# A softmax mixture: the last four groups' stores in two queues, from a freed slot, with the last copy in two pieces

## The chip, the cores and the metric

The kernel runs on one core of a Trainium2 chip. The metric is device time in microseconds (us) of one execution. Three runs of the kernel before took 794.04, 794.33 and 794.41 us, a median of 794.33 us. The profile was taken of a further execution that took 794.6 us.

Five engines work beside each other, each through its own list of instructions in order: TensorE (PE, matrix products; PEld is its load of weights), VectorE (DVE), ScalarE (ACT), GpSimd (POOL) and SyncE (SP). SP does nothing here but issue transfers (DMAs); ACT can issue them too, between its own instructions. Transfers issued by SP show in the trace as queue q1, those issued by ACT as queue q10. "SPq" and "ACTq" are instructions of those two that issue or wait.

## The reference

For each of 32 x 128 = 4096 rows there are four heads of 4096 logits and four prior values. Each head goes through a softmax of its own, and the four are averaged with the softmax of the priors as weights:

```python
prior_probs = softmax(prior, axis=-1)                 # [32, 128, 4]
softmax_h   = softmax(logits, axis=-1)                # [32, 128, 4, 4096]
mixture     = (prior_probs[..., None] * softmax_h).sum(axis=2)   # [32, 128, 4096], float32
```

The logits are 268 MB and the output is 67 MB, all in float32.

## The kernel before

**Units and groups.** The 4096 rows are cut into 32 groups (g) of 128 rows, and each group into two units of 64 rows, so there are 64 units, n = 0 to 63. A unit's logits are one tile of 128 partitions by 2 x 4096 numbers, 4 MB: a row takes two partitions, and each partition holds two of the row's heads (i = 0 and 1).

**A unit's way through the engines.** `load(n)` (L62) brings the 4 MB into one of five slots, slot n % 5; only the last unit comes as two loads of 2 MB, one per i. `top(n, i)` (L72) lets DVE find the row maximum of 4096 numbers (L74) and ACT take the exponential in place and its sum (L77). `weigh(n, i)` (L81) lets DVE invert the sum, POOL build a 128 x 64 weight matrix (L84), and PE multiply it with the slot in eight products of 512 columns (L91). The two `weigh` of a unit add up in one PSUM accumulator, `accs[n % 2]`. Its 128 partitions are not 128 rows: partitions 0 to 63 hold columns 0 to 2047 of the 64 output rows (c = 0), and partitions 64 to 127 hold columns 2048 to 4095 of the same rows (c = 1). `evict(n)` (L105) is an ACT copy of 128 x 2048 from PSUM to the group's place in SBUF, and `store(g)` (L108) sends a group out as two DMAs of 1 MB, one for c = 0 and one for c = 1. So every store reads one half of the partitions.

**Order.** The scheduling is written out by hand. In the loop (L148) unit n's `top` calls come ahead of the rest of unit w = n - 1:

```python
top(n, 0);  weigh(w, 1);  load(w + 5)      # SP waits until PE has read the whole slot of unit w
top(n, 1);  weigh(n, 0);  evict(w)
store(w // 2)                              # if w is odd
```

**Where a group's output waits.** `home(g)` (L100) says where a group is copied to. Up to group 29 that is `obuf`, with a place for even and one for odd groups. Groups 30 and 31 go to slot 4, (N - 5) % 5, which no unit after 59 uses.

**Which queue.** Groups 0 to 27 are stored from ACT (L109, `HOLD` = 28), right after the copy of their second unit. The last four groups are stored from SP. Groups 28 and 29 are held back: their four stores stand on SP behind the last load (L159 to L163). Group 30's follow after unit 61's copy. Group 31 goes out in two parts, its first unit's rows after unit 62's copy (L166) and its second unit's after the last copy (L169), each as two DMAs of 512 KB. On SP the tail is therefore one line: load 62, load 63 in two halves, then 28 (c = 0, c = 1), 29, 30, 31 first unit, 31 second unit, always c = 0 ahead of c = 1.

Of the kernel before, what the change touches and what calls it, by code (L numbers as in the profile page):

```python
# [1 line left out]

# [4 lines left out]

FP32 = mybir.dt.float32
AF = mybir.ActivationFunctionType
ALU = mybir.AluOpType  # L10
AX = mybir.AxisListType

P = 128
M = 64
J = 2
Q = 2
BANK = 512
SLOTS = 5


@with_exitstack
def kernel(
    ctx: ExitStack,
    tc: tile.TileContext,
    logits: bass.AP,
    prior: bass.AP,
    out: bass.AP,
):
    nc = tc.nc
    B, S, H, V = logits.shape  # L30
    R = M * J
    G = B * S // R
    N = G * J
    W = V // 2
    assert G * R == B * S and G == 32 and H == 2 * Q and V == 8 * BANK


    lg = logits.rearrange("b s h v -> (b s) h v").rearrange(
        "(g m j) (q i) v -> g j m q (i v)", m=M, j=J, i=Q
    )  # L40
    ov = out.rearrange("b s v -> (b s) v").rearrange("(g m j) v -> g m j v", m=M, j=J)
    pv = prior.rearrange("b s h -> (b s) h").rearrange("(g r) h -> g r h", r=R)

    cpool = ctx.enter_context(tc.tile_pool(name="cpool", bufs=1))
    psum = ctx.enter_context(tc.tile_pool(name="psum", bufs=1, space=bass.MemoryType.PSUM))

    slots = [cpool.tile([P, Q, V], FP32, name=f"slot{i}") for i in range(SLOTS)]

    obuf = cpool.tile([P, 2, J, W], FP32, name="obuf")
    accs = [psum.tile([P, W], FP32, name=f"acc{i}") for i in range(2)]  # L50

    sel = cpool.tile([P, M], FP32, name="sel")
    wts = [[cpool.tile([P, M], FP32, name=f"wt{k}{i}") for i in range(Q)] for k in range(2)]
    pr = cpool.tile([G, R, H], FP32, name="pr")
    pn = cpool.tile([G, J, Q, M, Q], FP32, name="pn")
    pmax = cpool.tile([G, R], FP32, name="pmax")
    pp = cpool.tile([P, J, Q, G], FP32, name="pp")
    nmax = [cpool.tile([P, N], FP32, name=f"nmax{i}") for i in range(Q)]
    dsum = [cpool.tile([P, N], FP32, name=f"dsum{i}") for i in range(Q)]
    rden = [cpool.tile([P, N], FP32, name=f"rden{i}") for i in range(Q)]  # L60

    def load(n):  # L62
        src = lg[n // J, n % J]
        if n < N - 1:
            nc.sync.dma_start(out=slots[n % SLOTS], in_=src)  # L65
        else:
            for i in range(Q):
                nc.sync.dma_start(
                    out=slots[n % SLOTS][:, i], in_=src[:, :, i * V : (i + 1) * V]
                )  # L70

    def top(n, i):  # L72
        x = slots[n % SLOTS][:, i]
        nc.vector.tensor_reduce(  # L74
            out=nmax[i][:, n : n + 1], in_=x, axis=AX.X, op=ALU.max, negate=True
        )
        nc.scalar.activation(  # L77
            x, x, AF.Exp, bias=nmax[i][:, n : n + 1], accum_out=dsum[i][:, n : n + 1]
        )

    def weigh(n, i):  # L81
        nc.vector.reciprocal(rden[i][:, n : n + 1], dsum[i][:, n : n + 1])  # L82
        wt = wts[n % 2][i]
        nc.gpsimd.tensor_scalar(  # L84
            out=wt, in0=sel, scalar1=rden[i][:, n : n + 1],
            scalar2=pp[:, n % J, i, n // J : n // J + 1], op0=ALU.mult, op1=ALU.mult,
        )

        for b in range(W // BANK):
            for c in range(2):  # L90
                nc.tensor.matmul(  # L91
                    accs[n % 2][c * M : (c + 1) * M, b * BANK : (b + 1) * BANK],
                    lhsT=wt,
                    rhs=slots[n % SLOTS][:, i, c * W + b * BANK : c * W + (b + 1) * BANK],
                    start=i == 0, stop=i == Q - 1,
                )

    HOLD = G - 4

    def home(g):  # L100
        if g < G - 2:
            return obuf[:, g % 2]
        return slots[(N - 5) % SLOTS][:, g % 2].rearrange("p (j w) -> p j w", j=J)

    def evict(n):  # L105
        nc.scalar.copy(home(n // J)[:, n % J], accs[n % 2])  # L106

    def store(g, js=slice(0, J)):  # L108
        eng = nc.scalar if g < HOLD else nc.sync  # L109
        for c in range(2):  # L110
            eng.dma_start(
                out=ov[g, :, js, c * W : (c + 1) * W], in_=home(g)[c * M : (c + 1) * M, js]
            )

    with tc.manual_schedule():
        for n in range(SLOTS):
            load(n)
        nc.scalar.dma_start(out=pr, in_=pv)

        nc.gpsimd.memset(sel, 1.0)  # L120
        nc.gpsimd.affine_select(  # L121
            out=sel, in_=sel, compare_op=ALU.is_ge, fill=0.0, base=0,
            pattern=[[-Q, M]], channel_multiplier=1,
        )
        nc.gpsimd.affine_select(  # L125
            out=sel, in_=sel, compare_op=ALU.is_ge, fill=0.0, base=Q - 1,
            pattern=[[Q, M]], channel_multiplier=-1,
        )

        nc.vector.reduce_max(pmax, pr, axis=AX.X)  # L130
        nc.vector.tensor_sub(pr, pr, pmax.unsqueeze(2).to_broadcast([G, R, H]))  # L131
        nc.scalar.activation(pr, pr, AF.Exp)  # L132
        nc.vector.reduce_sum(pmax, pr, axis=AX.X)  # L133
        nc.vector.reciprocal(pmax, pmax)  # L134
        prv = pr.rearrange("g (m j) (q i) -> g j i m q", j=J, i=Q)
        pmv = pmax.rearrange("g (m j) -> g j m", j=J)
        for j in range(J):
            for i in range(Q):
                nc.vector.tensor_mul(  # L139
                    pn[:, j, i], prv[:, j, i], pmv[:, j].unsqueeze(2).to_broadcast([G, M, Q])  # L140
                )
        pq = pn.rearrange("g j i m q -> g j i (m q)")
        for t in range(P // 32):
            nc.vector.transpose(  # L144
                pp[32 * t : 32 * (t + 1)], pq[:, :, :, 32 * t : 32 * (t + 1)]
            )

        for n in range(N):  # L148
            w = n - 1
            top(n, 0)  # L150
            if w >= 0:
                weigh(w, 1)
                if w + SLOTS < N:
                    load(w + SLOTS)
            top(n, 1)
            weigh(n, 0)
            if w >= 0:
                evict(w)
                if w == N - SLOTS:  # L159
                    for g in range(HOLD, w // J):  # L160
                        store(g)
                if w % J == J - 1 and (w // J < HOLD or w >= N - SLOTS):
                    store(w // J)  # L163

        n = N - 1
        store(n // J, slice(0, 1))  # L166
        weigh(n, 1)
        evict(n)
        store(n // J, slice(1, 2))  # L169


# [1 line left out]
_INS = ['logits', 'prior']  # L173
_OUTS = [((32, 128, 4096), 'float32')]


# [23 lines left out]
```

## Time and profile before

| What | Value |
|---|---|
| median of three runs | 794.33 us |
| profiled execution, whole | 794.6 us |
| its span (first to last instruction) | 792.9 us |
| outside the span | 1.7 us |
| busiest engines, share of the span | ACT 76%, DVE 72%, PE 69% |
| bytes moved | 268.5 MB read, 67.1 MB written |
| landing of load 62, the last 4 MB load | 754.57 us |
| end of the last ACT copy | 782.79 us |

How to read it: times are microseconds from the start of the span. Where a row shows an instruction and "x4", four like it follow each other, and the duration is that from the first one's start to the last one's end. The "DMA share" of a stretch is the mean busy share of the core's 16 DMA engines in it; it comes out a little over 1.00 at times, because packets are counted where they start. "To landing" is the time from a DMA's issue until its completion is signalled. The trace also holds every DMA packet with its start, duration, size and queue; a load's packet is 32 KB (16 KB for the two half loads), a store's is 8 KB.

### The profile page before, as it was taken

What the parts mean: (1) busy time and instruction counts of PE and PEld (TensorE: products, weight loads), DVE (VectorE), ACT (ScalarE), POOL (GpSimd) and SP (SyncE); (2) the same over time, 40 slices, a digit from 0 to 9 for tenths busy, and PEclk for the clock granted to TensorE, in tenths of its full rate; (3) what the DMA queues carried; (4) which work ended last, traced back from release to release, by engine and by line L of the source; (5) the groups of instructions that cost most, each with busy time, mean ns of one, the idle gap of its engine ahead of it and who ended that gap; (6) DMA issues with size and microseconds to landing.
All of it is one profiled execution on the core that took longest, in us unless ns stands there. A gap on an engine that the chain in (4) does not pass through costs nothing.

```text
span 792.9 us, 5418 instructions
## 1 busy us (share of the span) xinstructions
PE 544.3 (69%) x2048; PEld 159.6 (20%) x2048; DVE 573.3 (72%) x268; ACT 600.1 (76%) x322; POOL 51.1 (6%) x135
## 2 busy tenths in 40 slices
PE   0766567687776687666866677768568687776773
PEld 0212112122221122121211221212112122222221
DVE  5986867767768668677687686776866867767890
ACT  1897777787787787777877778778778777787893
POOL 0000000000000000000000000000000000000000
PEclk9998998877898977999799899887998877998998
DMA  9999999999999999999999999999999999999997
GB/s 375 441 414 431 430 426 429 433 431 428 433 436 433 434 434 431 429 427 437 429 431 429 431 434 431 433 436 430 433 432 432 427 432 427 432 431 438 432 386 234
DMA packets 18681, 335.95 MB, mean 424 GB/s; under 512 B 2112, under 2 KB 2112, under 8 KB 2144
## 3 DMA queue, kind: packets, MB, share of 16 engines
q1 hardware_dynamic: 10544, 276.83, 81.9%
q10 hardware_dynamic: 8112, 58.79, 17.6%
q8 instruction: 16, 0.26, 0.1%
q14 instruction: 9, 0.07, 0.0%
HBM read 268.50 MB, written 67.11 MB: 423 GB/s over the span
## 4 chain that ended last, share of the span: by engine, by line
DMA 76%; PE 10%; DVE 10%; issue 1%; POOL 1%; ACT 1%; SPq 0%; POOLq 0%
DMA slot<-in_logits_dram 76%; PE acc L91 10%; DVE nmax L74 9%; POOL wt L84 1%; ACT slot L77 0%; ACT slot L106 0%; SPq L65 0%; DVE rden L82 0%; POOLq L84 0%
## 5 line engine op out<-in xcount | busy, mean ns | idle before, releaser
L91 PE MATMUL acc<-slot,wt 128*64 128x512 f32 x2048 | 544.3, 689 | 236.6 <-POOL wt L84 236.5
L74 DVE TENSOR_REDUCE nmax<-slot 128x1 f32<-128x4096 f32 x128 | 563.5, 4410 | 194.6 <-DMA slot<-in_logits_dram 194.6
L77 ACT ACTIVATE slot<-slot,nmax 128x4096 f32<-128x4096 f32 x128 | 474.6, 3708 | 177.1 <-DVE nmax L74 175.7
L91 PEld LDWEIGHTS acc<-slot,wt 128*64 128x64 f32 x2048 | 159.6, 157 | 620.4 <-POOL wt L84 315.4
L106 ACT COPY obuf<-acc 128x2048 f32<-128x2048 f32 x60 | 110.7, 1845 | 0.0
L84 POOL TENSOR_SCALAR wt<-sel,rden,pp 128x64 f32<-128x64 f32 x128 | 50.3, 393 | 725.3 <-DVE rden L82 725.3
L77 ACT ACTIVATION_READ_ACCUMULATOR slot<-slot,nmax 128x1 f32 x128 | 23.9, 187 | 0.0
L82 DVE RECIPROCAL rden<-dsum 128x1 f32<-128x1 f32 x128 | 19.6, 153 | 5.1 <-ACT slot L77 5.1
L106 ACT COPY slot<-acc 128x2048 f32<-128x2048 f32 x4 | 7.4, 1850 | 2.8 <-PE acc L91 2.8
L130 DVE TENSOR_REDUCE pmax<-pr 32x128 f32<-32x512 f32 x1 | 0.7, 673 | 2.7 <-DMA pr<-in_prior_dram 2.7
L132 ACT ACT_TABLE_LOAD x1 | 1.3, 1283 | 1.2 <-PEq L184 1.2
L132 ACT ACTIVATE pr<-pr 32x512 f32<-32x512 f32 x1 | 0.6, 629 | 1.6 <-DVE pr L131 1.6
L144 DVE STREAM_TRANSPOSE pp<-pn 32x128 f32<-32x128 f32 x4 | 1.2, 302 | 0.1
L133 DVE TENSOR_REDUCE pmax<-pr 32x128 f32<-32x512 f32 x1 | 0.7, 674 | 0.7 <-ACT pr L132 0.7
L134 DVE RECIPROCAL pmax<-pmax 32x128 f32<-32x128 f32 x1 | 0.9, 941 | 0.0
L139 DVE TENSOR_TENSOR pn<-pr,pmax 32x128 f32<-32x128 f32 x4 | 0.9, 274 | 0.0
L131 DVE TENSOR_TENSOR pr<-pr,pmax 32x512 f32<-32x512 f32 x1 | 0.7, 678 | 0.0
L121 POOL TENSOR_SCALAR_AFFINE_SELECT sel<-sel 128x64 f32<-128x64 f32 x1 | 0.2, 238 | 0.1
L125 POOL TENSOR_SCALAR_AFFINE_SELECT sel<-sel 128x64 f32<-128x64 f32 x1 | 0.2, 238 | 0.1
L120 POOL MEMSET sel<- 128x64 f32 x1 | 0.2, 151 | 0.3 <-POOLq L184 0.3
L184 POOL MEMSET const-float32-0.0<- 128x1 f32 x1 | 0.1, 98 | 0.3 <-issue 0.3
L184 POOL MEMSET const-bfloat16-1.0<- 128x1 bf16 x1 | 0.1, 101 | 0.0
(2 smaller groups left out, 0.2 us busy)
## 6 DMA issues: line engine op xcount, KB each, us to landing
slot<-in_logits_dram SPq DMA_DIRECT2D x63, 4096.0 KB, 38.0
out_dram<-obuf ACTq DMA_DIRECT2D x56, 1024.0 KB, 25.5
slot<-in_logits_dram SPq DMA_DIRECT2D x2, 2048.0 KB, 32.9
out_dram<-obuf SPq DMA_DIRECT2D x4, 1024.0 KB, 31.0
out_dram<-slot SPq DMA_DIRECT2D x2, 1024.0 KB, 15.5
out_dram<-slot SPq DMA_DIRECT2D x4, 512.0 KB, 9.2
pr<-in_prior_dram ACTq DMA_DIRECT2D x1, 64.0 KB, 1.8
```

The source lines that it names most:

```text
L74: nc.vector.tensor_reduce(out=nmax[i][:, n : n + 1], in_=x, axis=AX.X, op=ALU.max, negate=True)
L77: nc.scalar.activation(x, x, AF.Exp, bias=nmax[i][:, n : n + 1], accum_out=dsum[i][:, n : n + 1])
L82: nc.vector.reciprocal(rden[i][:, n : n + 1], dsum[i][:, n : n + 1])
L84: nc.gpsimd.tensor_scalar(out=wt, in0=sel, scalar1=rden[i][:, n : n + 1], scalar2=pp[:, n % J, i, n // J : n // J + 1], op0=ALU.mult, op1= ...
L91: nc.tensor.matmul(accs[n % 2][c * M : (c + 1) * M, b * BANK : (b + 1) * BANK], lhsT=wt, rhs=slots[n % SLOTS][:, i, c * W + b * BANK : c * ...
L106: nc.scalar.copy(home(n // J)[:, n % J], accs[n % 2])
L130: nc.vector.reduce_max(pmax, pr, axis=AX.X)
L131: nc.vector.tensor_sub(pr, pr, pmax.unsqueeze(2).to_broadcast([G, R, H]))
L132: nc.scalar.activation(pr, pr, AF.Exp)
L134: nc.vector.reciprocal(pmax, pmax)
L139: nc.vector.tensor_mul(pn[:, j, i], prv[:, j, i], pmv[:, j].unsqueeze(2).to_broadcast([G, M, Q]))
L144: nc.vector.transpose(pp[32 * t : 32 * (t + 1)], pq[:, :, :, 32 * t : 32 * (t + 1)])
```

## The change

It touches only the end of the kernel and the bookkeeping of slots.

1. **Four slots for the last six units.** Units 58 to 63 use the slots 4, 0, 1, 2, 4, 0. Before they used 3, 4, 0, 1, 2, 3. A load is issued once the unit that had its slot before is done (`prior_user`). Loads 58 to 63 thus wait for units 54 to 59, where they waited for 53 to 58.
2. **Homes.** Slot 3 is free after unit 53, and groups 28 and 29 are copied there. Groups 30 and 31 go to `obuf`. `obuf` has the same size as before under another shape.
3. **Two queues.** Each of the last stores' c = 0 halves goes out from SP and its c = 1 half from ACT. The c = 1 halves of groups 28 and 29 stand on ACT between `top(62, 0)` and `top(62, 1)`; their c = 0 halves stand on SP behind the last load. The halves of group 30 follow unit 61's copy, and those of group 31's first unit follow unit 62's copy. All of ACT's issues are in its own list: what stands behind them on ACT are the remaining exponentials and copies.
4. **The last copy in two pieces.** `evict(63)` is done as two ACT copies of 128 x 1024, and after each its columns are stored, 256 KB from SP and 256 KB from ACT.

In the built program ACT gains six DMA issues and one copy in its list, SP goes from ten DMAs behind the last load to six, all of them c = 0 halves, and PE, DVE and POOL keep their instructions and order. Each of the four final stores waits for one of the stores of groups 28 and 29 to complete, because it uses that store's completion semaphore again.

```diff
-    obuf = cpool.tile([P, 2, J, W], FP32, name="obuf")
+    obuf = cpool.tile([P, J, V], FP32, name="obuf")
...
+    def slot(n):
+        return slots[n % SLOTS if n < N - 6 else (4, 0, 1, 2)[(n - N + 6) % 4]]
...
+    def part(eng, g, c, js=slice(0, J), lo=0, hi=W):
+        eng.dma_start(
+            out=ov[g, :, js, c * W + lo : c * W + hi],
+            in_=home(g)[c * M : (c + 1) * M, js, lo:hi],
+        )
...
     def home(g):
-        if g < G - 2:
-            return obuf[:, g % 2]
-        return slots[(N - 5) % SLOTS][:, g % 2].rearrange("p (j w) -> p j w", j=J)
+        x = slots[3] if HOLD <= g < G - 2 else obuf
+        return x[:, g % 2].rearrange("p (j w) -> p j w", j=J)
-    def evict(n):
-        nc.scalar.copy(home(n // J)[:, n % J], accs[n % 2])
-    def store(g, js=slice(0, J)):
-        eng = nc.scalar if g < HOLD else nc.sync
+    def evict(n, lo=0, hi=W):
+        nc.scalar.copy(home(n // J)[:, n % J, lo:hi], accs[n % 2][:, lo:hi])
+    def store(g):
         for c in range(2):
-            eng.dma_start(
-                out=ov[g, :, js, c * W : (c + 1) * W], in_=home(g)[c * M : (c + 1) * M, js]
-            )
+            part(nc.scalar, g, c)
+    def prior_user(n):
+        return max(k for k in range(n) if slot(k) is slot(n))
...
             top(n, 0)
+            if n == N - 2:
+                for g in (HOLD, HOLD + 1):
+                    part(nc.scalar, g, 1)
             if w >= 0:
                 weigh(w, 1)
-                if w + SLOTS < N:
-                    load(w + SLOTS)
+                for k in range(SLOTS, N):
+                    if prior_user(k) == w:
+                        load(k)
+                if w == N - 3:
+                    for g in (HOLD, HOLD + 1):
+                        part(nc.sync, g, 0)
             top(n, 1)
             weigh(n, 0)
             if w >= 0:
                 evict(w)
-                if w == N - SLOTS:
-                    for g in range(HOLD, w // J):
-                        store(g)
-                if w % J == J - 1 and (w // J < HOLD or w >= N - SLOTS):
-                    store(w // J)
+                g = w // J
+                if w % J == J - 1 and g < HOLD:
+                    store(g)
+                elif w == N - 3 or w == N - 2:
+                    js = slice(0, J) if w == N - 3 else slice(0, 1)
+                    part(nc.sync, g, 0, js)
+                    part(nc.scalar, g, 1, js)
         n = N - 1
-        store(n // J, slice(0, 1))
         weigh(n, 1)
-        evict(n)
-        store(n // J, slice(1, 2))
+        for lo in (0, W // 2):
+            evict(n, lo, lo + W // 2)
+            part(nc.sync, n // J, 0, slice(1, 2), lo, lo + W // 2)
+            part(nc.scalar, n // J, 1, slice(1, 2), lo, lo + W // 2)
```

## The prediction, made before the changed kernel ran

> **What bounds the kernel now.** I read the page's 40 slices first, then its chain of the work that ended last.
>
> ```profile
> DMA  9999999999999999999999999999999999999997
> GB/s 375 441 414 431 430 426 429 433 431 428 433 436 433 434 434 431 429 427 437 429 431 429 431 434 431 433 436 430 433 432 432 427 432 427 432 431 438 432 386 234
> ...
> DMA 76%; PE 10%; DVE 10%; issue 1%; POOL 1%; ACT 1%; SPq 0%; POOLq 0%
> ```
>
> The DMA engines are busy throughout, at about 430 GB/s, and the chain is mostly loads. So the bytes set the time, and no change at the end can gain more than the end loses. It loses in the last two slices, 386 and 234 GB/s: with 19.8 us a slice, 19.8 x (1 - 386/432) + 19.8 x (1 - 234/432) = 2.1 + 9.1 = 11.2 us. The table of stretches shows how (the columns after ACT and POOL are PE clock, DMA share, GB/s).
>
> ```profile
> core 0: us, PE busy (x) PEld busy (x) DVE busy (x) ACT busy (x) POOL busy (x), PEclk, DMA share, GB/s
> 755.00:760.00 5.00, 3.33 (x18) 0.95 (x16) 5.00 (x3) 5.00 (x4) 0.39 (x1) 1.00 1.00 423
> ...
> 765.00:769.00 4.00, 3.27 (x18) 0.94 (x16) 4.00 (x3) 4.00 (x4) 0.39 (x1) 1.00 1.01 354
> 769.00:773.00 4.00, 3.15 (x16) 0.84 (x12) 3.33 (x2) 4.00 (x3) 0.00 (x0) 1.00 1.03 344
> 773.00:777.00 4.00, 3.47 (x16) 1.06 (x16) 0.17 (x1) 4.00 (x3) 0.62 (x2) 1.00 0.96 320
> 777.00:783.00 6.00, 3.84 (x18) 1.06 (x16) 0.00 (x0) 2.99 (x2) 0.17 (x1) 1.00 0.92 276
> 783.00:786.00 3.00, 0.00 (x0) 0.00 (x0) 0.00 (x0) 0.00 (x0) 0.00 (x0) 0.99 0.99 259
> 786.00:793.00 7.00, 0.00 (x0) 0.00 (x0) 0.00 (x0) 0.00 (x0) 0.00 (x0) 0.50 0.39 132
> ```
>
> From 765 us on the engines are as busy as before but move less: 354 falling to 259 GB/s. Only stores are left then. In the trace's packets the last load packet ends at 764.26 and the last store packet at 791.45. Of the 8.39 MB of the held groups 28 to 31, 0.66 MB has started by 764.26; the other 7.73 MB take 27.2 us, or **284 GB/s**. 27% of these 8 KB packets took over 500 ns, with a cluster near 630, twice the usual 309. Earlier, as store packets ran singly between load packets, 98% of 7168 took 312 ns or less. So packets get in each other's way when all engines read one half of the partitions at a time. The tail is bound by these stores: ACT is done at 782.79, and 8 us of stores follow.
>
> The compute path of the tail is ACT's list (start, duration, work, and in brackets the wait ahead of it):
>
> ```profile
> 759.18 3.71 ACT L77 ACTIVATE slot<-slot,nmax 128x4096 f32<-128x4096 f32 x1
> 762.79 0.19 ACT L77 ACTIVATION_READ_ACCUMULATOR slot<-slot,nmax 128x1 f32 x1
> 763.43 3.71 ACT L77 ACTIVATE slot<-slot,nmax 128x4096 f32<-128x4096 f32 x1 [0.45 <-DVE nmax L74]
> ...
> 767.14 1.84 ACT L106 COPY slot<-acc 128x2048 f32<-128x2048 f32 x1
> 768.89 3.71 ACT L77 ACTIVATE slot<-slot,nmax 128x4096 f32<-128x4096 f32 x1
> ...
> 776.28 1.84 ACT L106 COPY slot<-acc 128x2048 f32<-128x2048 f32 x1
> 780.92 1.87 ACT L106 COPY slot<-acc 128x2048 f32<-128x2048 f32 x1 [2.79 <-PE acc L91]
> ```
>
> These are units 62 and 63. From 763.43 to 776.28 ACT never waits, so whatever is put into its list there comes out at the end.
>
> **The change, part by part.**
>
> *Four slots: nothing.* Each load from 58 on is issued one unit later. In this trace load 62 is issued at 721.74, when unit 57 is done, and load 63's second half at 733.6, when unit 58 is. Afterwards load 62 goes at 733.6 and load 63's second half near 745. Loads land at 735.1, 744.9, 754.6 (units 60 to 62), so load 62's bytes start to flow at 744.9 and those of 63's second half near 759.9. The cover is 11 and 15 us of load already queued. If it were gone, each us short would cost a us. A gain is excluded, since no load goes earlier.
>
> *Homes: nothing.* Slot 3 is read last at 674.2 (unit 53), and its first copy comes after 711. `obuf`'s last ACT stores have landed by 733, its next copy comes at 757.
>
> *28 and 29 in two queues.* ACT issues two DMAs behind the exponential that ends at 762.98. Two such issues take 1.20 us in this kernel (the pair at 677.07). They end at 764.2 where the next exponential began at 763.43: **+0.8**. The trace shows no issue behind work it need not wait for. If ACT issues ahead, this is 0 and the stores may go as early as 749.5, when unit 59's copy ends; in four-to-one packet turns with the loads they would then hold up load 62 by some 1.1 us. Bounds 0 to +1.1. Issued at 763, they also share the engines with load 63's second half for its last 1.5 us; that half then lands near 766, and DVE reads it at 767.77, so this costs nothing.
>
> *30 on ACT.* The issue follows the copy that ends at 768.98 and pushes the last two exponentials: **+0.7** (0.60 and a hand-over). The spread of an issue is wide:
>
> ```profile
> L111 SPq DMA_DIRECT2D out_dram<-slot x6: 466/1231/2299, 769.0 to 783.3; - x6
> ```
>
> On SP in this very stretch three issues of the six, each the second of a pair, took 1.9 to 2.3 us. On ACT they would stand alone, so I take 0.6; the other end is 2.3, +1.7 more for group 30 and as much for the last copy's first piece. Group 31's first unit issues behind the copy that ends at 778.1, inside the 2.79 us wait: nothing, as long as it is shorter than that.
>
> *Copy in two pieces.* No half copy is in the trace. It costs between half of 1.87 and all of it; 4096 numbers take 3.71, 2048 take 1.85, so time goes by size and I take 1.0. PE's last product ends at 780.9 + 1.5 = 782.4. Piece one ends at 783.4, ACT's issue at 784.05, piece two at 785.05, against 782.79 before: **ACT ends 2.3 us later.**
>
> *The stores.* If two queues let packets of both halves alternate, they run at the 423 to 432 GB/s of the mixed stretches: 28 and 29 (4.19 MB) are through by 774.5, 30 (2.10 MB, ready at 770.4) by 779.5, 31's first unit (1.05 MB, issued at 779.7) by 784. The completions that the final stores wait for are those of 28 and 29: 774.5, or 779 at 284 GB/s, ahead of 783.4, so this wait, which on ACT has piece two behind it, costs nothing. Then nothing is in the way of the end: last issue 785.1; 1.45 us to its first packet (the kernel's first load: issue 0.80, packet 2.25); 0.52 MB in 1.2 us at 424 or 2.0 at 260, I take 1.7, and 0.3 for what piece one left: 788.5. From the last packet to the end of the span this trace has 792.9 - 791.45 = 1.45. **Span 789.95, or 2.95 us shorter.** The profiled execution becomes 794.6 - 2.95 = 791.65; the median stands 0.27 below it: **791.4 us.**
>
> [...] The trace's row is 284 GB/s for halves one behind the other. [...]
>
> **Rivals.**
>
> 1. *The queues gain little (same).* The stores still end last, at 270 to 300 GB/s, or ACT's issues take 2.3 us. At 300 the span is 764.3 + 25.8 + 1.45 = 791.5, at 270 it is 794.4, and with 3.4 us of slow issues on my forecast 793.3. With the 1.45 us between a span and the median (1.7 - 0.27) that is 792.9 to 795.8 us. For it: ACT's and SP's DMAs use the same 16 engines, and these are already at share 1.0. Against it: their packets are slow only when they meet.
> 2. *The halves meet in step (slower).* With strict turns, two engines that start on the same half stay on it together, packet after packet, where the single queue lets a fast engine run ahead to the other half. It decides below 284 GB/s (8192 bytes x 16 engines / 284 = a mean packet of 461 ns). At 250 GB/s the span is 764.3 + 30.9 + 1.45 = 796.6, so **798.1 us**; at 212, every packet at 618 ns, 803.6. For it: the rate sank toward 259 as the tail went on. Against it: in the steady part store packets took turns with load packets on all engines and hardly ever met.
> 3. *Loads run dry with four slots.* Against it are 11 us of cover; a gap of 3 us would end the gain at 794.4. Counted with the first.
>
> **How the numbers follow.** 0.2%, or 1.6 us, is about what a measurement of this kernel can tell from no change: 792.7 to 795.9. Forecast, 0.58: from 789.9 (pair hidden on ACT, 1.2 us transfer, nothing left of piece one) to 792.7. First rival, 0.17. Second, 0.25, from 795.9 to 803.6; I count some two fifths of it below 797. The range from 789.9 to 797 leaves out about 0.15 above and 0.03 below. The forecast's own range is 789.9 to 792.7.
>
> **What would show it.** Right: over 400 GB/s in the first 8 us after the last load packet, store packets at 309 ns, then gaps in the DMA share near 780; ACT's last piece ending near 785, and the last landing within 4 us of its issue. Slower rival: share near 1 to the end, packets of 500 to 630 ns on both queues. Wrong in the cheap parts: DVE waiting longer than 0.9 us for load 61 or 62, or an ACT gap over 1 us behind a DMA issue. The forecast is wrong if the last store packets wait behind others at 785.

## The result, and the profile after

Nine runs of the changed kernel took 790.95 to 793.28 us, a median of **792.9 us**; nine of the kernel before on the same chip had a median of 794.33. The ratio is **0.9974, 95% interval [0.9964, 0.9985]**: faster, by 1.4 us where 2.9 were forecast. The nine times fall in two groups, 790.95 to 792.08 (four runs) and 792.9 to 793.28 (five). The profiled execution took 793.28 us, so it is of the slower group; its span is 791.6 us, where 789.95 was forecast.

The page of the changed kernel, rates by slice (19.8 us each) and the chain of waits:

```profile
GB/s 376 442 416 431 431 428 430 432 431 427 434 432 435 429 432 436 430 433 431 434 429 433 431 431 429 428 435 431 429 431 432 431 432 433 433 430 436 429 416 229
...
DMA 73%; PE 12%; DVE 10%; ACT 2%; issue 1%; POOL 1%; ACTq 0%; SPq 0%; POOLq 0%
```

The slice before the last has risen from 386 to 416 GB/s, the last has stayed at 229 (234 before). In the chain DMA has lost 3% of the span and PE and ACT have gained it: the chain now leaves the stores earlier and runs through the last products and copies. The table of stretches (PE clock, DMA share and GB/s are the last three columns) shows where:

```profile
765.00:769.00 4.00, 3.27 (x16) 0.92 (x14) 4.00 (x3) 4.00 (x3) 0.40 (x1) 1.00 1.01 422
769.00:773.00 4.00, 3.26 (x16) 0.86 (x12) 3.28 (x1) 3.29 (x2) 0.00 (x0) 1.00 1.02 391
773.00:777.00 4.00, 2.55 (x8) 0.83 (x10) 0.16 (x1) 4.00 (x3) 0.40 (x1) 0.76 0.99 356
777.00:783.00 6.00, 6.00 (x26) 1.78 (x22) 0.16 (x1) 2.04 (x3) 0.40 (x1) 0.88 0.74 197
783.00:786.00 3.00, 0.23 (x2) 0.00 (x0) 0.00 (x0) 2.02 (x2) 0.00 (x0) 0.88 0.68 182
786.00:791.60 5.60, 0.00 (x0) 0.00 (x0) 0.00 (x0) 0.00 (x0) 0.00 (x0) 0.50 0.56 163
```

From 765 to 769 the stores run at 422 GB/s where they ran at 354, and from 777 on the DMA share is 0.74 where it was 0.92: the stores now wait for the compute path. In that path, the PE clock of 0.76 from 773 to 777 is new (it was 1.00).

ACT's timeline of the changed kernel (start, duration, work, and in brackets the idle time ahead and what ended it):

```profile
759.25 0.55 ACTq L101 DMA_DIRECT2D out_dram<-slot  x1
759.35 3.71 ACT L79 ACTIVATE slot<-slot,nmax 128x4096 f32<-128x4096 f32 x1
759.90 0.79 ACTq L101 DMA_DIRECT2D out_dram<-slot  x1
...
763.54 3.71 ACT L79 ACTIVATE slot<-slot,nmax 128x4096 f32<-128x4096 f32 x1 [0.39 <-DVE nmax L76]
...
769.12 0.58 ACTq L101 DMA_DIRECT2D out_dram<-obuf  x1
769.80 3.71 ACT L79 ACTIVATE slot<-slot,nmax 128x4096 f32<-128x4096 f32 x1 [0.71 <-ACT obuf L113]
...
779.07 0.52 ACTq L101 DMA_DIRECT2D out_dram<-obuf  x1
783.28 1.01 ACT L113 COPY obuf<-acc 128x1024 f32<-128x1024 f32 x1 [4.24 <-PE acc L93]
784.32 0.52 ACTq L101 DMA_DIRECT2D out_dram<-obuf  x1
784.88 1.01 ACT L113 COPY obuf<-acc 128x1024 f32<-128x1024 f32 x1 [0.59 <-ACT obuf L113]
785.92 0.50 ACTq L101 DMA_DIRECT2D out_dram<-obuf  x1
```

The two issues of groups 28 and 29 (759.25 and 759.90) lie beside the exponential that starts at 759.35, and the next one starts at 763.54 (763.43 before): they cost nothing. ACT's issues are thus not bound to the gaps between its instructions: the first one goes out 0.1 us before the exponential that stands ahead of it in the list has begun. Group 30's issue, which has to wait for the copy ahead of it, costs the forecast 0.7. The first piece then waits 4.24 us for PE, where the copy waited 2.79 before. PE's timelines show why. The last 16 products (32 matmul records) of the kernel before:

```profile
773.53 7.34 PE L91 MATMUL acc<-slot,wt 128*64 128x512 f32 x32 [1.38 <-POOL wt L84]
```

and of the changed kernel, which starts them 0.92 us later and takes 1.44 us longer:

```profile
774.45 8.78 PE L93 MATMUL acc<-slot,wt 128*64 128x512 f32 x32 [2.19 <-POOL wt L86]
```

Cut at the ends of the low clock, the changed kernel's table of stretches reads:

```profile
771.63:775.04 3.41, 1.22 (x8) 0.30 (x6) 0.81 (x2) 3.41 (x3) 0.40 (x1) 1.00 1.00 351
775.04:778.45 3.41, 3.41 (x12) 0.99 (x10) 0.16 (x1) 3.41 (x3) 0.40 (x1) 0.50 0.90 348
778.45:783.20 4.75, 4.75 (x22) 1.32 (x20) 0.00 (x0) 0.59 (x1) 0.00 (x0) 1.00 0.71 166
```

After 3.41 us in which PE was busy for 1.22 only, it was granted half its clock for the next 3.41 us. The 1.44 us that the products take longer are those 3.41 us, in which PE did the work of 1.97. The last section says why only some executions show it.

### The profile page after: what moved, and what is told of

Its sections match the earlier page's. It is cut to its first block, busy times and chain, and to the rows that moved or that the text cites. A ratio compares the mean times of both kernels' runs of the same rounds, so it can differ in the third digit from the quotient of the medians.

```text
span 791.6 us, 5426 instructions
## 1 busy us (share of the span) xinstructions
PE 548.0 (69%) x2048; PEld 160.4 (20%) x2048; DVE 573.3 (72%) x268; ACT 600.2 (76%) x323; POOL 51.6 (7%) x135
## 4 chain that ended last, share of the span: by engine, by line
DMA 73%; PE 12%; DVE 10%; ACT 2%; issue 1%; POOL 1%; ACTq 0%; SPq 0%; POOLq 0%
DMA slot<-in_logits_dram 73%; PE acc L93 12%; DVE nmax L76 10%; ACT slot L79 1%; POOL wt L86 1%; ACT obuf L113 1%; ACTq L101 0%; DVE rden L84 0%; SPq L70 0%; POOLq L86 0%; ACTq L79 0%; ACTq L113 0%
## 5 line engine op out<-in xcount | busy, mean ns | idle before, releaser
L113 ACT COPY obuf<-acc 128x2048 f32<-128x2048 f32 (+1 forms) x61 | 110.9, 1817 | 4.8 <-PE acc L93 4.2
```

The costliest lines, as they stand in the source:

```text
L113: nc.scalar.copy(home(n // J)[:, n % J, lo:hi], accs[n % 2][:, lo:hi])
```

## The experiments

**Theory.** (A) The gain comes from two queues that read opposite halves: in the 6 us after the last load packet 2% of the store packets take over 500 ns, 16% before the change. What is left of the forecast was lost on the compute path: group 30's issue on ACT pushes PE's last products past a 2.2 us gap, after which PE sometimes gets half its clock for 3.41 us, and this makes the two groups of times. **Rivals.** The gain comes from the free slot, the homes or the split; or from a second queue as such, whatever it reads; and the loss is in the stores.

All of these kernels compute the whole output. Ratios are against the kernel before, run beside them on the same chip: a median of 794.55 us beside e1, e3, e4 and e5, of 794.43 beside e0, e3b, e6 and e8, and of 794.29 beside e2 and e9.

| Kernel | median us (lowest to highest) | ratio, 95% interval |
|---|---|---|
| e1 all from SP | 794.78 (794.54 to 795.1) | 1.0004 [0.9995, 1.0013] |
| e9 both queues on the same half | 795.74 (795.25 to 796.12) | 1.0018 [1.0009, 1.0027] |
| e0 the changed kernel again | 791.6 (791.12 to 793.1) | 0.9968 [0.9956, 0.9981] |
| e3 eight products more | 792.28 (791.94 to 792.38) | 0.9972 [0.9961, 0.9983] |
| e3b four products more | 791.52 (791.4 to 791.69) | 0.9962 [0.9949, 0.9976] |
| e4 group 30 issued later | 791.76 (791.56 to 792.09) | 0.9966 [0.9953, 0.9978] |
| e5 group 31 from SP | 791.94 (791.48 to 792.12) | 0.9967 [0.9954, 0.9979] |
| e6 first piece copied early | 791.3 (790.92 to 791.65) | 0.996 [0.9947, 0.9972] |
| e2 last copy whole | 792.57 (792.05 to 793.98) | 0.9981 [0.9973, 0.999] |
| e8 e4, e5 and e6 together | 790.83 (790.6 to 791.53) | 0.9955 [0.9942, 0.9967] |

### e1: one queue again

Slots, homes and pieces stay as changed; every store of groups 28 to 31 goes out from SP.

```diff
-                    part(nc.scalar, g, 1, js)
+                    part(nc.sync, g, 1, js)
...
-            part(nc.scalar, n // J, 1, slice(1, 2), lo, lo + W // 2)
+            part(nc.sync, n // J, 1, slice(1, 2), lo, lo + W // 2)
```

(and the c = 1 halves of 28 and 29 behind their c = 0 halves on SP.)

> All stores of groups 28 to 31 go out from SP in one queue, c = 0 ahead of c = 1; the four slots, the homes and the last copy in two pieces stay as in the changed kernel. Theory A (the gain comes from the two queues): after the last load the rate falls back to about 284 GB/s, the last store packet ends near 791.5, and the median is 794.0 to 794.6, like the kernel before. Rival B (the gain comes from the copy in two pieces or from the order, not from the second queue): the median stays at 792.9 or below.

The whole gain is gone (ratio 1.0004). Its table of stretches:

```profile
765.00:769.00 4.00, 3.27 (x16) 0.92 (x14) 4.00 (x3) 4.00 (x4) 0.39 (x1) 1.00 1.02 354
769.00:773.00 4.00, 2.83 (x14) 0.72 (x10) 3.01 (x2) 4.00 (x3) 0.18 (x1) 1.00 1.01 336
773.00:777.00 4.00, 3.70 (x18) 1.10 (x18) 0.16 (x1) 4.00 (x3) 0.61 (x2) 1.00 0.99 315
777.00:783.00 6.00, 3.61 (x16) 1.01 (x16) 0.00 (x0) 2.79 (x3) 0.00 (x0) 1.00 0.89 269
```

354, 336, 315 and 269 GB/s are the kernel before's numbers within 8. ACT is done at 782.6 with nothing pushed and the last store packet still ends at 791.70. So the four slots, the homes and the split gain nothing by themselves; it takes the second queue.

### e9: two queues on the same half

Two DMAs change places: SP takes both halves of group 28, ACT both of group 29, each c = 0 first.

```diff
-                for g in (HOLD, HOLD + 1):
-                    part(nc.scalar, g, 1)
+                for c in range(2):
+                    part(nc.scalar, HOLD + 1, c)
...
-                    for g in (HOLD, HOLD + 1):
-                        part(nc.sync, g, 0)
+                    for c in range(2):
+                        part(nc.sync, HOLD, c)
```

> Groups 28 and 29 still go out in two queues, but each queue takes both halves of one group one behind the other: SP sends group 28, c = 0 then c = 1, and ACT sends group 29, c = 0 then c = 1. Everything else is the changed kernel, and all of the output is computed. Both queues thus read the same half for part of the time: ACT's starts early, beside load 63, so I reckon with some 2 us in which both read c = 0, 3 us with opposite halves, and 2 us in which both read c = 1. Theory A (packets are slow when two engines read the same half at once, so it is the halves that matter and not the number of queues): in the 6 us after the last load packet a good part of the packets, 20% or more, takes over 500 ns, against 4% or fewer in the changed kernel, and the rate is 330 to 390 GB/s instead of 414 to 438; the stores of groups 28 and 29 end 1 to 2 us later. The time stays within 1 us of the changed kernel's, because gaps in the DMA share near 780 take it up. Theory B (two queues keep the engines busy whatever they read): 414 GB/s or more and 309 ns packets as in the changed kernel.

In the 6 us after the last load packet 26% of the store packets take over 500 ns (2% in the changed kernel) and the rate is 335 GB/s (423). That is what Theory A expected. What I had not expected is that it goes on. Its table of stretches:

```profile
765.00:769.00 4.00, 3.27 (x16) 0.92 (x14) 4.00 (x3) 3.63 (x3) 0.39 (x1) 1.00 1.02 317
769.00:773.00 4.00, 2.80 (x14) 0.72 (x10) 2.82 (x1) 3.66 (x2) 0.00 (x0) 1.00 1.00 297
773.00:777.00 4.00, 3.02 (x14) 1.05 (x16) 0.30 (x2) 4.00 (x5) 0.39 (x1) 1.00 0.95 231
777.00:783.00 6.00, 4.29 (x20) 1.06 (x16) 0.03 (x1) 2.62 (x3) 0.39 (x1) 1.00 0.86 249
```

The rate sinks to 231 GB/s. Packets, put to their DMAs by their order in each queue (mean duration in ns):

| DMA | changed kernel | e9 |
|---|---|---|
| SP, first | 28 c = 0: 760.7 to 767.5, 309 | 28 c = 0: 760.5 to 768.4, 357 |
| ACT, first | 28 c = 1: 763.0 to 768.2, 312 | 29 c = 0: 762.6 to 768.7, 367 |
| SP, second | 29 c = 0: 767.2 to 773.3, 336 | 28 c = 1: 767.8 to 776.5, 472 |
| ACT, second | 29 c = 1: 767.9 to 773.0, 328 | 29 c = 1: 768.3 to 775.8, 464 |
| SP, third | 30 c = 0: 772.7 to 779.6, 365 | 30 c = 0: 776.1 to 784.5, 440 |
| ACT, third | 30 c = 1: 772.6 to 780.3, 350 | 30 c = 1: 775.1 to 784.3, 462 |

My reckoning of 2 us together, 3 apart and 2 together was wrong: the queues stay together for all of both DMAs, and when the halves become opposite (group 30) the packets stay slow. The median is 4.3 us above the changed kernel's faster group (791.4) and 2.7 above its slower one (793.0), not within 1 us, and above the kernel before's. A second queue as such is no gain here; what counts in these runs is that the queues take opposite halves. Both queues on one half is the state that the prediction's second rival feared. It is real, and the changed kernel's pairing keeps clear of it until some 773 us (422 and 391 GB/s, against 317 and 297 in e9); here the order of the DMAs brings it about. That queues which begin on opposite halves fall into step by themselves, that a single queue lets a fast engine run ahead to the other half, or that group 30's packets stay slow because engines once in step remain so, is argued, not shown: a packet's record names no engine. One more thing is open: every store that reads partitions 0 to 63 also writes the left half of the output's columns, so no run here tells whether the packets meet at the partitions that they read or at the addresses that they write.

### e0: the changed kernel again

> The changed kernel once more, beside the next three on one chip. Theory A (PE's clock falls in the gap ahead of unit 63's products in some executions and not in others, because the clock is set by stretches of 3.4 us that run free of the kernel): two groups of times, near 791.2 and 793.0, or one of them alone, and a spread over 1 us. Rival B (the times differ from chip to chip): a spread below 0.6 us, about a level of its own.

Five runs: 791.12, 791.41 and 791.6, then 792.81 and 793.1. With the nine above, the changed kernel has 7 runs from 790.95 to 792.08 and 7 from 792.81 to 793.28, and none between. The profiled execution (793.1 us) is of the slower group, and its last products again take 8.78 us, behind a gap of 2.18. No profile caught an execution of the faster group.

### e3 and e3b: PE kept busy in the gap

Ahead of unit 63's products PE does eight (e3) or four (e3b) others, whose results are overwritten by unit 63's first products. e3b has range(W // BANK // 2) for the first loop.

```diff
+            if n == N - 1:
+                for b in range(W // BANK):
+                    for c in range(2):
+                        nc.tensor.matmul(
+                            accs[n % 2][c * M : (c + 1) * M, b * BANK : (b + 1) * BANK],
+                            lhsT=wts[w % 2][1],
+                            rhs=slot(w)[:, 1, c * W + b * BANK : c * W + (b + 1) * BANK],
+                            start=True, stop=True,
+                        )
             top(n, 1)
```

> The changed kernel with eight more products (1.8 us) on PE in the gap ahead of unit 63's, into the accumulator that unit 63 overwrites; they read data that is there and need nothing new, so only PE's idle time changes, from 2.2 to 0.4 us. Theory A (the gap lets PE's granted clock fall to 0.5 for 3.4 us in some executions, which makes the last 16 or 32 products up to 1.5 us longer): the slow executions go, all runs lie between 790.9 and 791.6, and the granted clock is 1.00 from 774 to 783. Rival B (runs differ because of the stores): the spread of 790.95 to 793.28 stays, median 792.9.

The low clock was gone and the seven times lay within 0.44 us, but at 792.28, above Theory A's 790.9 to 791.6: the eight products took 3.60 us, twice what I had reckoned, and moved unit 63's products to 775.27, about 1 us late. So e3b, with half of them:

> As the run with eight more products on PE ahead of unit 63's, but with four: there eight took 3.65 us and not the 1.8 that was expected of them, and so pushed unit 63's products back by 1 us. Four take 1.8 us and fit in the gap of 2.2. Theory A (the gap costs clock): granted clock 1.00 from 772 to 783 in the profile, ACT's first piece 1.4 us earlier than in the changed kernel's profile, all times within 0.8 us of each other, median 791.0 to 791.6. Rival B (the last stores set the end, whatever PE does): 792.3 as with eight.

```profile
771.80 1.89 PE L172 MATMUL acc<-slot,wt 128*64 128x512 f32 x8
774.15 7.35 PE L93 MATMUL acc<-slot,wt 128*64 128x512 f32 x32 [0.47 <-POOL wt L86]
```

These are e3b's PE rows: a gap of 0.47 instead of 2.19, and the last products take 7.35 us as before the change. All five times lie from 791.4 to 791.69; the slower group is gone. Work that nobody needs made the kernel's median no slower, and its times steady. The low clock is thus shown to be the cause of the two groups, as far as twelve runs without a slow one show it. (In e5 and e6 below the profiled execution has the low clock too, and five times each lie within 0.64 and 0.73 us, so for them it is not known how many of the executions had it.)

### e4: group 30 issued behind the last exponential

```diff
             top(n, 1)
+            if n == N - 1:
+                part(nc.scalar, G - 2, 1)
...
-                    part(nc.scalar, g, 1, js)
+                    if w == N - 2:
+                        part(nc.scalar, g, 1, js)
```

> The changed kernel with group 30's c = 1 store issued on ACT behind unit 63's second exponential, ahead of unit 62's copy, so that it no longer stands ahead of unit 63's two exponentials. Theory A (ACT's list is on the path that sets the end): ACT's last copy ends 0.7 us earlier, PE's gap falls from 2.2 to 1.5 us so that its clock falls less often, and the median is 790.2 to 791.5. Rival B (the stores set the end, so that issuing half of group 30 some 8 us later costs): 793.5 or more, since group 30's c = 0 half then runs alone at 618 ns a packet.

The issue no longer has the copy right ahead of it in ACT's list, and it costs nothing: it goes out at 771.88 for 0.54 us, before the exponential ahead of it in the list begins at 772.25. PE's gap is 1.38 again and its products take 7.35. ACT's last issue is at 783.23, 2.7 us earlier than in the changed kernel, but the last store packet only 1.5 us earlier, at 788.49, 5.3 us behind its issue. Stores are again what ends last, as these stretches of e4's table show with a DMA share of 0.96 and 0.91:

```profile
773.00:777.00 4.00, 3.77 (x18) 1.18 (x20) 0.16 (x1) 4.00 (x3) 0.53 (x2) 1.00 0.96 274
777.00:783.00 6.00, 3.54 (x16) 0.94 (x16) 0.00 (x0) 2.62 (x3) 0.00 (x0) 1.00 0.91 274
```

The median of 791.76 is 0.3 us above Theory A's range and 1.7 below rival B's. So with the compute path as short as before, the stores themselves end near 788: the changed kernel sits where both limits are within some 2 us of each other.

### e5: group 31 from SP alone

```diff
-                    part(nc.scalar, g, 1, js)
+                    part(nc.scalar if w == N - 3 else nc.sync, g, 1, js)
...
-            part(nc.scalar, n // J, 1, slice(1, 2), lo, lo + W // 2)
+            part(nc.sync, n // J, 1, slice(1, 2), lo, lo + W // 2)
```

> The changed kernel with all of group 31's stores from SP, c = 0 ahead of c = 1; groups 28 to 30 stay in two queues. Theory A (where the DMA engines are idle when two stores arrive, the two queues' halves run one behind the other anyway, all engines on c = 0 first): no loss from one queue there; the issues that leave ACT (0.5 us between the two pieces) weigh against SP's second issue (0.5 us), so within 0.5 us of the changed kernel. Rival B (two queues run the halves side by side here too): the last 1 MB takes twice as long, 2 us later, 794.5 or more.

791.94 us: nothing is lost by one queue here. The profiled execution has the low clock (8.78 us), and the last packet ends at 789.09, 0.9 us earlier than in the changed kernel. Some 0.4 of that is an earlier start (the copies begin at 782.88 instead of 783.28), and ACT makes both pieces in 1.93 us with no issue between them. The packets of the changed kernel show that a second queue brings nothing here: group 31's first unit was issued on both queues at 779.07, when the engines had nearly run empty (a DMA share of 0.29 from 778 to 780); from 780.3 to 782.3 only SP's packets ran, 653 ns each, and from 782.3 to 784.3 all but one were ACT's, 458 ns. From nearly idle engines the halves went one behind the other, at 225 to 234 GB/s. In e5, from one queue, they look the same: c = 0 from 779.8 to 782.6 at 645 ns, c = 1 from 782.4 to 784.6 at 447.

### e6: the first piece copied while PE still works

The accumulator becomes two tiles of 1024 columns, so that the first piece need not wait for the last four products.

```diff
-    accs = [psum.tile([P, W], FP32, name=f"acc{i}") for i in range(2)]
+    accs = [[psum.tile([P, W // 2], FP32, name=f"acc{i}{h}") for h in range(2)] for i in range(2)]
...
-        weigh(n, 1)
-        for lo in (0, W // 2):
-            evict(n, lo, lo + W // 2)
+        def out(b):            # called behind column block b's products
+            if b % 2:
+                lo = (b - 1) * BANK
+                evict(n, lo, lo + W // 2)
...
+        weigh(n, 1, out)
```

> The changed kernel with each accumulator as two tiles of 1024 columns, and the first piece of unit 63's copy and its stores ahead of the last four of its products, so that it no longer waits for all of them. Every copy is then two of 1024. Theory A (the last issue sets the end, with 4.4 us behind it): the first piece is copied 1 to 1.8 us earlier beside PE, ACT's last copy ends 1.0 to 1.6 us earlier, and so does the kernel, by 0.8 to 1.5 us against the changed kernel. Rival B (the last megabyte's stores set the end, 1.05 MB at 230 GB/s from the first piece on): the gain follows the first piece's issue, 1.0 to 1.8 us.

791.3 us. In its profiled execution PE has the low clock (8.78 us), and still the first piece starts at 781.38 and the second at 783.10, each right behind its own products; the last packet ends at 788.23, 1.8 us earlier than in the changed kernel. The first piece's issue moved by 1.9 us and the last copy's end by 1.8, so this run does not tell the two theories apart.

### e2: the last copy whole

```diff
-        for lo in (0, W // 2):
-            evict(n, lo, lo + W // 2)
-            part(nc.sync, n // J, 0, slice(1, 2), lo, lo + W // 2)
-            part(nc.scalar, n // J, 1, slice(1, 2), lo, lo + W // 2)
+        evict(n)
+        part(nc.sync, n // J, 0, slice(1, 2))
+        part(nc.scalar, n // J, 1, slice(1, 2))
```

> The changed kernel with the last copy whole (128 x 2048), followed by one store of 512 KB from each of SP and ACT. The output is computed in full. Theory A (the split lets the first half of the last unit's bytes go while the second is copied): the copy ends near 784.1 with PE at the low clock or 782.7 without, against 785.9 and 784.4 for the second piece, because one issue and one hand-over between the pieces is saved (1.7 us earlier). The last 1.05 MB then go one half behind the other from idle engines, at about 225 GB/s: first packet 1.9 us after the issue, 4.7 us of packets, so the last packet ends about 6.6 us after the issue, against 4.1 after the last issue of the changed kernel: 0.8 us later in all, 0.2 to 1.4 us slower than the changed kernel. Rival theory (the split only adds an issue and a hand-over and nothing is gained by it): the same time as the changed kernel or up to 1 us faster.

Again two groups: six runs from 792.05 to 792.57 and five from 793.5 to 793.98. Median against median (792.4 and 791.4, 793.7 and 793.0) they lie 1.0 and 0.7 us above the changed kernel's groups, on another chip with the same time before (794.29 against 794.33 and 794.43). The split is worth some 0.8 us, as Theory A expected. In the profile the copy ends at 784.53 and the last packet at 790.41, 5.9 us behind the issue, where it is 4.1 in the changed kernel.

### e8: e4, e5 and e6 together

> The early copy, group 30's c = 1 store behind unit 63's second exponential, and all of group 31's stores from SP, together. Theory A: the gains of the first two add up as far as the stores let them: ACT done near 782.5 with PE at full clock, then 1.05 MB at 230 to 270 GB/s behind what is left of group 30 and of group 31's first unit; median 790.0 to 791.2. Rival B (the stores from the last load on are the bound again once ACT is this early, 7.7 MB at an average of 330 GB/s): 791.2 to 792, no better than with group 30 late alone.

**790.83 us, ratio 0.9955 [0.9942, 0.9967]**, the lowest median here, 0.45% under the kernel before and within Theory A's 790.0 to 791.2. Its interval overlaps those of the changed kernel, in both of its measurements, and of e3 to e6, so it is not shown to be faster than these. ACT's last piece ends at 781.77, 4.1 us earlier than in the changed kernel, but the last packet only 2.5 us earlier, at 787.57. The stores are the bound again, as rival B had it, though the time is below B's 791.2; e8's table shows the stores (268 GB/s at a share of 0.95):

```profile
773.00:777.00 4.00, 3.63 (x16) 1.06 (x16) 0.16 (x1) 4.00 (x3) 0.70 (x2) 1.00 0.97 293
777.00:783.00 6.00, 3.67 (x18) 1.06 (x16) 0.00 (x0) 3.05 (x4) 0.00 (x1) 1.00 0.95 268
```

## Why the prediction was right, and where its sizes were off

The sign and the mechanism held. The median of 792.9 us lies inside the range from 789.9 to 797, but 0.2 us outside the forecast's own, which ends at 792.7: the gain of 1.4 us is about half of what was forecast, and less than the 1.6 us that the prediction took as the least to tell from no change. (The interval says that it is a gain, and e0's median of 791.6 lies inside the forecast's own range. The prediction's three chances make 1.00, so the 0.03 that it puts below its range is in none of them.) The sum was short by 1.65 us of span (791.6 against 789.95), which comes apart by its own steps:

- *Four slots and homes: nothing.* Right. Load 62 landed at 754.68 (754.57 before), DVE waited 0.85 and 0.83 us for loads 61 and 62. The 0.11 shows on in ACT's list.
- *28 and 29 on ACT: +0.8.* Too high: 0. ACT issues past a running exponential (759.90, inside the one that starts at 759.35), the end 0 of the bounds. e4 and e8 show the same with group 30's issue (771.88 and 772.00, inside exponentials that start at 768.55 and 768.72).
- *30 on ACT: +0.7.* Right: 0.71 idle and the issue at 769.12.
- *PE's end at 782.4.* This term failed. It took the last products as a block of fixed length that only moves. They started 0.92 later, not 1.5, but took 8.78 us instead of 7.34: PE ended 0.83 later than forecast. The prediction looked at ACT's order for what is late next, and not at what a longer gap does to PE's clock. In the faster group this is, by e3b, not there. The trace of the kernel before had such a gap, over a hundred microseconds earlier, with the same 8.78 us behind it:

```profile
655.66 8.78 PE L91 MATMUL acc<-slot,wt 128*64 128x512 f32 x32 [2.14 <-POOL wt L84]
```

- *Pieces of 1.0 each.* Right: 1.01 and 1.01, issue between them 0.59. ACT ended at 785.89 for 785.05; the 0.84 is PE's.
- *From the last issue to the last packet, 3.4 us.* It was 4.1 (785.92 to 790.02). The first packet came 1.67 us after the issue (1.45 forecast), and the last piece took 2.4 (1.7, and 0.3 for the rest of piece one). Its two halves did run beside each other, in packets of 4 KB, which the split makes half as large, but the engines were busy for 0.68 of the time from 788 to 790 (231 GB/s). Why they were not busier is open.
- *From the last packet to the end, 1.45.* 1.58.

0.84 + 0.7 + 0.13 makes the 1.65 up to rounding. In the faster group, spans of 789.2 to 790.3 were measured. That the forecast's 789.95 is met there is luck in part: PE's start was put some 0.6 too late, since the pair of issues cost nothing, and the last stores 0.7 too short.

*The first 8 us at over 400 GB/s* came true in the mean (413), and for 6 us throughout (438, 414, 418 in steps of 2 us, then 381; 98% of the packets under 500 ns for 6 us). The rate then goes to 340, 376 and 328, a mean still over the 304 to 315 of one queue, so 424 GB/s for group 30's 2.10 MB was too high: its last packet ended at 780.3, not 779.5. It cost nothing, being covered by PE's end. The gap near 780 came (a share of 0.29 from 778 to 780); the last landing, put within 4 us of its issue, took 4.4 to 4.6.

*Two queues against one.* The two queues gave 422 GB/s where one gave 354 in the same 4 us of e1: 19% more. The stores of group 31 still went one half behind the other (653 ns packets of one queue, then 458 ns of the other); groups 28 and 29 did not, with both queues' packets side by side at 309 to 336 ns.

*The rivals.* The median falls into the first rival's range, from 792.7 on, by 0.2 us, but not for its reasons: in the first 6 us after the last load packet the two queues give the 423 GB/s that the forecast reckoned with, and no ACT issue of the changed kernel took over 0.8 us. The second did not occur in the main stretch, and e9 shows how near it was: two DMAs in another order, and the kernel is slower than before. The third did not occur.

## What to carry to other kernels

When only transfers that touch half of the partitions are left, it can pay to send the two halves in two queues so that at any time each queue reads the other half (422 GB/s here, where one queue gave 354); check it by the packet durations, since here two queues on the same half were slower than one (231 GB/s from 773 to 777 in e9, 315 in e1). Before a transfer is issued from a compute engine's list, see whether it must wait for the instruction right ahead of it: if so it held the list up by 0.7 us here, if not it ran beside it. When something pushes an engine that ends the kernel, look at the gap it opens on TensorE and not only at the order: here 0.8 us of gap more cost 1.4 us of clock, in half of the executions by their times.

## What the runs showed of the hardware that was not expected

- **In these traces PE's granted clock changed only in steps of 3.413 us, and went with how long PE had been busy in the 3.413 us before.** In each of the twelve traces the granted clock changes only at times that lie a whole number of 3.413 us apart, and this grid lies elsewhere in the kernel from execution to execution: carried back to the start of the span, it begins at 0.87 us in the kernel before and at 0.22 us in the changed one. Cut along it, the twelve traces have 1981 stretches at full clock. Of the 541 with under 1.38 us of PE work every one was followed by half the clock, of the 1383 with over 1.48 none, and of the 57 between 14. Of 681 stretches at half clock, the 543 with over 2.71 us of work were followed by the full clock and the 138 with under 2.70 by half the clock again.

  This settles why the low clock comes in some executions only. The gap of 2.18 to 2.25 us ahead of the last products fell whole into one stretch in the five profiles that have the low clock (changed, e0, e2, e5 and e6, with 1.20 to 1.23 us of work in that stretch; in e6 all but 0.04 us of the gap). In e9 the grid cut the same gap in two at 772.31, and both stretches kept enough work for the full clock behind them:

```profile
768.89:772.31 3.42, 2.91 (x14) 0.72 (x10) 2.93 (x1) 2.97 (x1) 0.00 (x0) 1.00 1.01 309
772.31:775.72 3.41, 1.74 (x8) 0.63 (x10) 0.16 (x1) 3.41 (x3) 0.39 (x1) 1.00 1.01 245
775.72:779.13 3.41, 3.37 (x18) 1.03 (x16) 0.17 (x1) 2.86 (x3) 0.39 (x1) 1.00 0.79 204
```

  The gaps of 1.38 to 1.44 (before, e1, e4, e8) leave 1.98 us or more in every stretch. As an estimate from these numbers, a stretch must hold 1.93 to 2.03 us of a gap of 2.18, which it does in 45 to 51% of the grid's positions; 7 of the changed kernel's 14 runs are in the slower group.
- **A product of 128x512 in float32 is two matmul records**: e3's eight products are 16 records in 3.60 us, 0.45 us a product.
- **Two queues on the same half were slower than one queue**: 231 GB/s in e9 from 773 to 777, 315 in e1.
- **From nearly idle engines two halves issued at the same time went one behind the other** (group 31's first unit), at 225 to 234 GB/s, with packets of 653 ns while one queue ran alone.
